# A new order and pace of the interleaved streams in a two-layer hybrid attention kernel

## The chip, the cores and the metric

One core of one Trainium2 chip. The metric is the device time of one execution in microseconds (us), the median over runs. The engines are TensorE (PE; its weight loads are PEld), VectorE (DVE), ScalarE (ACT), GpSimd (POOL, hardly used here) and SyncE (SP, on whose queue all loads and stores of this kernel are issued).

## The reference

A stack of two layers (D = 1024) over 512 latent tokens and 256 context tokens, weights shared between both. Each layer does this, and all of it is float32:

```python
h  = modulate(rms_norm(x, g_norm1[l]), sh1, sc1)      # latent; hc likewise from ctx
fl = stream_features(h, lw, rope)                     # one projection, split three ways
fc = stream_features(hc, lw, None)
mix_l, mix_c = token_mixers(fl, fc, lw, lam, lam_init, with_ctx_out)
x  = x + gt1 * (mix_l @ w_out[l])
x  = x + gt2 * swiglu(modulate(rms_norm(x, g_norm2[l]), sh2, sc2), w_gate, w_up, w_down)
```

`token_mixers` joins three groups of heads: four heads of latent attention with low-rank compressed q and kv (MLA), four heads of differential attention (softmax of one score matrix less lambda times softmax of a second), and eight heads of a bidirectional gated linear recurrence (HGRN) in chunks of 64 tokens, whose output is multiplied by a gate. Latent queries read context and latent keys; context queries read context alone. Layer 0 also computes the context's own output (`with_ctx_out`); layer 1 computes latent rows only.

## The kernel before

Activations lie transposed in SBUF, features on partitions and the 768 tokens along the free side (256 context, then 512 latent). Every float32 product is made of three fp32r matmuls, high*high, high*low and low*high (`gemm`, L189 to L198, the matmul is L195); so each weight block is fetched by SP into a staging tile `wst` (three buffers, L183), split by ACT into `whi` (L102) and by DVE into `wlo` (L105), and then used.

`phase_a(l, h, fs)` (L422) does everything of a layer up to the second norm. It runs four streams, each a Python generator that emits a piece of work and yields its estimated length:

- **g**, `stream_g`: the wide projections, in the order of the table `G_ORDER[l]`. `t0` to `t3` are the three HGRN projections of a pair of heads, `h0` and `h1` HGRN values, `q` differential q and k with rotary (DVE instructions of L105 on tiles `zt` and `raw_`), `d` differential values, `g0` to `g3` the HGRN gates (tanh on ACT, L105/L108 on DVE), `a4` to `a9` blocks of the modulation vector (their weights go through `wst` as well, L313). After them comes the output projection (L597 on).
- **h**, `stream_hh`: the recurrence, two heads at a time as two sub-streams. Its DVE work is the level products on tiles KK and QQ (L972), `copy_predicated` into the scores sc (L982), the chunk totals tot (L105), and the state scan sb (L108). A head pair's result is multiplied by its gate and stored in the scratch `scr_m`, slots 4 to 7; if the gate comes later than the pair, the `gate` step of g does it.
- **p**, `stream_p`: MLA compression, keys and values.
- **a**, `stream_a`, which starts when p has ended: softmax attention in items of 128 queries of one head. An item's scores (L775) go to a reduce on DVE (L779), an exponential on ACT into P, a reciprocal (L783), transposes of P on TensorE (L815), and the product with v (L829). Its results go to `scr_m`, slots 0 to 3. Attention units come in the order MLA context queries, MLA first latent batch, differential context, differential first latent batch, then the last 256 latent tokens.

Which stream emits next is decided by virtual time: each stream has a clock, the one furthest behind goes on, and its clock advances by the yielded length times the stream's pace. `PRM[l]` holds p's start offset and the paces of g, h, p and a. The tile scheduler then lays every engine's instructions out by priority, which falls with the order of emission; `AHEAD[l]` moves the priority of a stream's instructions by so many places. The order on each engine is fixed before the kernel runs.

The output projection goes over two batches of columns (layer 0: B1, the first 512 tokens, and B2, the last 256; layer 1: L1, latent tokens in the first 512 columns, and B2). For a batch it fetches two weight blocks, loads the eight slots of `scr_m` into one tile m2 as each becomes ready, and then makes eight column blocks:

```python
for k in (4, 5, 6, 0, 1, 2, 3, 7):
    yield from need(...)
    load(m2[:, k], scr_m[l][k, :, :, cols]...)
...
gemm(g[:, :n], w, [m2[:, :, i].bitcast(F32R) for i in range(2)], slice(0, n))
```

The matmuls take the slots in the order 0 to 7. For B2 the stream first waits for the end of stream a, so as to open its tile in the place that stream a's pool leaves.

After phase A come the feed-forward layer, then layer 1, then the final norm.

## Time and profile before

| | us |
|---|---|
| median of 3 runs | 2206.95 (2202.46 to 2211.0) |
| the profiled execution, its own time | 2209.03 |
| its span in the trace | 2206.9 |
| busy: TensorE, weight loads, VectorE, ScalarE | 2032.4, 1759.1, 1605.8, 1060.0 |
| mean granted clock of TensorE, share of full | 0.944 |
| layer 0's phase A | about 40 to 708 |
| layer 1's phase A | about 1280 to 1840 |

The profile comes from one execution; its span leaves out 2.1 us that the device's own time includes. A busy time is the time in which an engine has an instruction in hand, so a TensorE at a lower clock is busy for longer with the same work. The granted clock is the share of TensorE's full rate that the chip allowed in a stretch. Matmuls of one group overlap in the listing: starts are closer together than the lengths say.

### The profile page before, as it was taken

What the parts mean: (1) busy time and instruction counts of PE and PEld (TensorE: products, weight loads), DVE (VectorE), ACT (ScalarE), POOL (GpSimd) and SP (SyncE); (2) the same over time, 40 slices, a digit from 0 to 9 for tenths busy, and PEclk for the clock granted to TensorE, in tenths of its full rate; (3) what the DMA queues carried; (4) which work ended last, traced back from release to release, by engine and by line L of the source; (5) the groups of instructions that cost most, each with busy time, mean ns of one, the idle gap of its engine ahead of it and who ended that gap; (6) DMA issues with size and microseconds to landing.
All of it is one profiled execution on the core that took longest, in us unless ns stands there. A gap on an engine that the chain in (4) does not pass through costs nothing. (4 is left out here: it accounts for less than half of the span.)

```text
span 2206.9 us, 38015 instructions
## 1 busy us (share of the span) xinstructions
PE 2032.4 (92%) x14863; PEld 1759.1 (80%) x14863; DVE 1605.8 (73%) x3395; ACT 1060.0 (48%) x1871; POOL 13.1 (1%) x48
## 2 busy tenths in 40 slices
PE   7999899888898999999999999978988699999998
PEld 4887778666678888999999878757866489899997
DVE  5574597888657565797776776798568668877787
ACT  4433778565654323232333454445677444344443
POOL 0000000000000000000000000000000000000000
PEclk7999999888999999999999999989988589999999
DMA  9426744455765424464322333354645263333321
GB/s 318 122 77 165 196 131 131 128 164 170 223 203 167 125 86 153 129 187 132 118 70 68 118 114 102 95 150 128 171 129 163 83 204 98 96 105 101 103 85 68
DMA packets 321243, 296.51 MB, mean 134 GB/s; under 512 B 28875, under 2 KB 263721, under 8 KB 321065
## 3 DMA queue, kind: packets, MB, share of 16 engines
q1 hardware_dynamic: 321064, 294.10, 45.5%
q8 instruction: 117, 1.92, 0.4%
q14 instruction: 62, 0.50, 0.1%
HBM read 241.09 MB, written 52.95 MB: 133 GB/s over the span
## 5 line engine op out<-in xcount | busy, mean ns | idle before, releaser
L102 ACT ACTIVATE whi<-wst 128x1024 fp32r<-128x1024 f32 (+2 forms) x248 | 225.1, 908 | 399.9 <-PE f L195 146.4
L105 DVE TENSOR_TENSOR wlo<-wst,whi 128x1024 fp32r<-128x1024 f32 (+2 forms) x248 | 256.0, 1034 | 80.3 <-ACT whi L102 77.3
L195 PE MATMUL q<-hh,whi 128*128 128x384 f32 (+1 forms) x708 | 222.9, 317 | 4.3 <-ACT whi L102 3.2
L195 PE MATMUL q<-hh,wlo 128*128 128x384 f32 (+1 forms) x708 | 221.2, 315 | 0.9 <-DVE wlo L105 0.9
L195 PE MATMUL q<-hl,whi 128*128 128x384 f32 (+1 forms) x708 | 221.7, 314 | 0.0
L195 PE MATMUL g<-hh,whi 128*128 128x512 f32 (+1 forms) x560 | 199.6, 359 | 10.2 <-ACT zt L102 5.0
L195 PE MATMUL g<-hh,wlo 128*128 128x512 f32 (+1 forms) x560 | 197.8, 355 | 2.1 <-DVE wlo L105 2.1
L195 PE MATMUL g<-hl,whi 128*128 128x512 f32 (+1 forms) x560 | 198.9, 357 | 0.7 <-DVE hl L108 0.5
L195 PE MATMUL f<-ah,whi 128*128 128x512 f32 (+1 forms) x380 | 137.3, 364 | 5.3 <-DVE xT L108 4.1
L779 DVE TENSOR_REDUCE mx<-b 128x1 f32<-128x768 f32 (+1 forms) x120 | 101.5, 848 | 55.3 <-PE b L775 54.4
L195 PEld LDWEIGHTS q<-hh,whi 128*128 128x128 f32 x708 | 134.3, 190 | 9.1 <-ACT whi L102 5.1
L195 PE MATMUL f<-ah,wlo 128*128 128x512 f32 (+1 forms) x380 | 136.1, 361 | 1.1 <-DVE wlo L105 1.1
L195 PE MATMUL f<-al,whi 128*128 128x512 f32 (+1 forms) x380 | 136.5, 361 | 0.0
L108 DVE SCALAR_TENSOR_TENSOR xT<-f,mod,xT 128x256 f32<-128x256 f32 (+1 forms) x164 | 85.9, 546 | 69.1 <-PE f L195 68.5
L195 PEld LDWEIGHTS q<-hh,wlo 128*128 128x128 f32 x708 | 134.3, 190 | 1.7 <-DVE wlo L105 1.6
L195 PEld LDWEIGHTS q<-hl,whi 128*128 128x128 f32 x708 | 134.7, 191 | 0.3
L195 PEld LDWEIGHTS g<-hh,whi 128*128 128x128 f32 x560 | 108.1, 193 | 26.6 <-ACT zt L102 6.1
L102 ACT ACTIVATE kz<-KK 64x384 f32<-64x384 f32 (+1 forms) x192 | 91.3, 476 | 76.1 <-DVE KK L972 55.9
L775 PE MATMUL b<-k,q 96*128 96x256 f32 x352 | 100.5, 399 | 25.8 <-DMA q<-scr_d 15.6
L195 PEld LDWEIGHTS g<-hh,wlo 128*128 128x128 f32 x560 | 107.4, 192 | 17.2 <-DVE wlo L105 3.3
L195 PE MATMUL g<-T,whi 128*128 128x384 f32 (+1 forms) x544 | 121.1, 311 | 0.0
L195 PE MATMUL g<-m,whi 128*128 128x256 f32 (+1 forms) x512 | 117.2, 323 | 4.2 <-ACT acc L102 2.0
(308 smaller groups left out, 5021.2 us busy)
## 6 DMA issues: line engine op xcount, KB each, us to landing
wst<-in_w_in_dram SPq DMA_DIRECT2D x58, 512.0 KB, 5.3
wa<-in_w_ada_dram SPq DMA_DIRECT2D x56, 512.0 KB, 3.8
wst<-in_w_out_dram SPq DMA_DIRECT2D x32, 512.0 KB, 5.5
wst<-in_w_ffn_down_dram SPq DMA_DIRECT2D x64, 256.0 KB, 2.9
wst<-in_w_ffn_gate_dram SPq DMA_DIRECT2D x26, 512.0 KB, 3.7
wst<-in_w_ada_dram SPq DMA_DIRECT2D x24, 512.0 KB, 4.9
hin<-scr_z SPq DMA_DIRECT2D x48, 192.0 KB, 3.4
k<-scr_k SPq DMA_DIRECT2D x16, 576.0 KB
```

The source lines that it names most:

```text
L102: return S.activation(out=out, in_=in_, func=func, **kw)
L105: eng.tensor_tensor(out=out, in0=in0, in1=in1, op=op)
L108: return V.scalar_tensor_tensor(out=out, in0=in0, scalar=scalar, in1=in1, op0=op0, op1=op1)
L195: PE.matmul(out=o, lhsT=x[:, k, ms], rhs=y[:, k, cols], start=start and k == 0 and p == 0, stop=stop and k == nk - 1 and p == 2, skip_grou ...
L775: PE.matmul(out=s[:, 256 + k0:256 + k0 + kn], lhsT=qq[:, q0:q0 + 128], rhs=kk[:, k0:k0 + kn], start=p == 0, stop=p == len(passes) - 1)
L779: V.tensor_reduce(out=mx, in_=sv, axis=AX.X, op=ALU.min)
```

## The change

The tables that order the work have other numbers, and the output projection is written differently.

```diff
-G_ORDER = ("t0 h0 q t1 d t2 h1 t3 a5 a4 g0 a8 a6 g1 a9 a7 g3 g2", "t0 t1 h0 t2 q d h1 t3 g0 g1 g3 g2")
-PRM = ((40, 2, 2.1, 2, 1.2), (45, 1.8, 2.7, 2.2, 0.4))
+G_ORDER = ("t0 q t1 h0 d t2 h1 t3 a8 a5 a4 a6 g1 a9 g0 a7 g2 g3", "t0 h0 t1 t2 q d h1 g3 t3 g0 g1 g2")
+PRM = ((40, 2.4, 2.1, 2, 0.91), (35, 1.8, 2.7, 2.2, 0.4))
-AHEAD = ({}, {})
+AHEAD = ({'h': 0, 'a': 80}, {'a': 40, 'h': -40})
...
-                    if cols is B2:
+                    if cols is B2 and full:
                         yield from need("a")
                         op = apool.enter_context(tc.tile_pool(name=f"Q{l}", bufs=1, reuse_waits="tile"))
+                    order = [4, 5, 6, 0, 1, 2, 7, 3]
...
-                    m2 = op.tile([128, KT, 2, n], F32, name="m2")
-                    for k in (4, 5, 6, 0, 1, 2, 3, 7):
+                    m2 = op.tile([128, len(order), 2, n], F32, name=f"m2_{cols.start}")
+                    rows = {}
+                    for i, k in enumerate(order):
                         yield from need(...)
-                        load(m2[:, k], scr_m[l][k, :, :, cols].rearrange("i p t -> p i t"))
+                        load(m2[:, i], scr_m[l][k, :, :, cols].rearrange("i p t -> p i t"))
+                        rows[k] = [m2[:, i, e:e + 1].bitcast(F32R) for e in range(2)]
...
-                        gemm(g[:, :n], w, [m2[:, :, i].bitcast(F32R) for i in range(2)], slice(0, n))
+                        for k in rows:
+                            gemm(g[:, :n], [t[:, k:k + 1] for t in w], rows[k], slice(0, n), start=k == order[0], stop=k == list(rows)[-1])
```

In layer 0 the step `q` comes before `h0`, the modulation blocks a8 a5 a4 a6 follow one another, and the gates g0, g2 and g3 come later. In layer 1 `h0` comes before `t1` and the gate g3 before `t3`. Stream g's pace number in layer 0 goes from 2 to 2.4 (its clock runs faster, so it emits later), stream a's from 1.2 to 0.91 (it emits earlier). Stream p starts earlier in layer 1. In both layers stream a's instructions get a higher priority, in layer 1 those of h a lower one. Layer 1's second batch of the output projection no longer waits for stream a: it has a tile of its own beside the first batch's. The slots lie in the tile in the order of their loading, with 7 before 3, and the matmuls take them in that order, where they went from 0 to 7. A branch for a missing eighth slot is written too, which the order of eight slots never enters. The number of matmuls and of VectorE instructions is the same. The lines of the rest of the code lie seven further down (L779 becomes L786).

What moves is seen in the order of the instructions on an engine. VectorE, layer 1, where the first softmax reduce stands; before:

```order
L105 TENSOR_TENSOR zt<-zt,cosT 128x512
L972 TENSOR_TENSOR KK<-KK,tot 64x48x8
L105 TENSOR_TENSOR zt<-zt 128x512
L972 TENSOR_TENSOR QQ<-QQ,tot 64x32x8
L972 TENSOR_TENSOR KK<-KK,tot 64x48x8
L972 TENSOR_TENSOR QQ<-QQ,tot 64x32x8
L105 TENSOR_TENSOR zt<-zt 128x768
L105 TENSOR_TENSOR tot<-tot 128x48
L982 COPY_PREDICATED sc<-masks_75,c 64x4x64 x2
L779 TENSOR_REDUCE mx<-b 128x1
L972 TENSOR_TENSOR KK<-KK,tot 64x192x2
L779 TENSOR_REDUCE mx<-b 128x1
```

and now:

```order
L105 TENSOR_TENSOR zt<-g,sinT 128x512
L105 TENSOR_TENSOR zt<-zt,cosT 128x512
L105 TENSOR_TENSOR QQ<-hin 128x512
L105 TENSOR_TENSOR zt<-zt 128x512
L979 TENSOR_TENSOR KK<-KK,tot 64x96x4 x2
L786 TENSOR_REDUCE mx<-b 128x1 x2
L105 TENSOR_TENSOR zt<-zt 128x768
L105 TENSOR_TENSOR tot<-tot 128x96
L105 TENSOR_TENSOR tot<-hin 128x384
```

The head stream's products (L972, now L979) that stood ahead of the reduces (L779, now L786) have gone behind them.

VectorE, layer 0, among the softmax rows of MLA's first latent batch; before:

```order
L972 TENSOR_TENSOR QQ<-QQ,tot 64x96x4
L972 TENSOR_TENSOR KK<-KK,tot 64x96x4
L972 TENSOR_TENSOR QQ<-QQ,tot 64x96x4
L105 TENSOR_TENSOR tot<-tot 128x96
L982 COPY_PREDICATED sc<-masks_75,c 64x6x64 x2
L105 TENSOR_TENSOR mixs<-mix,mixs 128x256
L779 TENSOR_REDUCE mx<-b 128x1
L972 TENSOR_TENSOR QQ<-QQ,tot 64x192x2
L972 TENSOR_TENSOR KK<-KK,tot 64x192x2
L972 TENSOR_TENSOR QQ<-QQ,tot 64x192x2
L982 COPY_PREDICATED sc<-masks_75,c 64x6x64
L783 RECIPROCAL z<-z 128x1
```

and now:

```order
L105 TENSOR_TENSOR wlo<-wst,whi 128x1024
L786 TENSOR_REDUCE mx<-b 128x1
L105 TENSOR_TENSOR mixs<-mix,mixs 128x256
L786 TENSOR_REDUCE mx<-b 128x1
L790 RECIPROCAL z<-z 128x1
L105 TENSOR_TENSOR wlo<-wst,whi 128x1024
L790 RECIPROCAL z<-z 128x1
L786 TENSOR_REDUCE mx<-b 128x1
L790 RECIPROCAL z<-z 128x1
L786 TENSOR_REDUCE mx<-b 128x1
```

The reduces and reciprocals follow one another with split weights (wlo) and stored results (mixs) between them; the KK, QQ and sc rows of a head pair, which stood there, come later.

TensorE, layer 0, the last attention rows ahead of the output projection, whose rows are those on m; before:

```order
L775 MATMUL b<-k,q 128x256
L775 MATMUL b<-k,q 128x512
L775 MATMUL b<-k,q 128x256
L775 MATMUL b<-k,q 128x512
L815 MATMUL c<-ident,P 128x128 x12
L775 MATMUL b<-k,q 128x256
L775 MATMUL b<-k,q 128x512
L829 MATMUL c<-pt,v 64x256 x12
L195 MATMUL g<-m_6626,whi 128x512 x2
```

and now:

```order
L782 MATMUL b<-k,q 128x256
L782 MATMUL b<-k,q 128x512
L195 MATMUL g<-hh,wlo 128x256
L195 MATMUL g<-hh,whi 128x256
L195 MATMUL g<-hl,whi 128x256
L195 MATMUL g<-hh,wlo 128x256
L195 MATMUL g<-m_0_6743,whi 128x512 x2
L195 MATMUL g<-m_0_6743,wlo 128x512
L195 MATMUL g<-m_0_6743,whi 128x512 x2
L195 MATMUL g<-m_0_6743,wlo 128x512
L822 MATMUL b<-ident,P 128x128 x6
L782 MATMUL b<-k,q 128x256
```

Rows of a gate's projection (g from hh, hl) now stand among the scores (L775, now L782), and the first rows of the output projection (on m_0) come ahead of transposes and scores that in the order before had all gone by then.

## Rows read from the trace of the kernel before

**Rows 1.** The page: busy time of each engine, its share of the span, and instructions.

```profile
PE 2032.4 (92%) x14863; PEld 1759.1 (80%) x14863; DVE 1605.8 (73%) x3395; ACT 1060.0 (48%) x1871; POOL 13.1 (1%) x48
```

**Rows 2.** Stretches of layer 0's phase A: length, then busy time by engine, clock, DMA.

```profile
core 0: us, PE busy (x) PEld busy (x) DVE busy (x) ACT busy (x) POOL busy (x), PEclk, DMA share, GB/s
...
237.00:333.00 96.00, 91.60 (x961) 78.18 (x960) 71.16 (x157) 72.42 (x138) 0.59 (x4) 1.00 0.55 152
333.00:430.00 97.00, 91.38 (x926) 74.95 (x926) 78.31 (x213) 70.63 (x140) 0.58 (x4) 0.96 0.38 112
430.00:480.00 50.00, 40.49 (x366) 31.74 (x362) 35.39 (x87) 31.86 (x56) 0.29 (x2) 0.77 0.58 163
480.00:551.00 71.00, 59.43 (x620) 42.61 (x621) 61.90 (x147) 41.32 (x77) 0.29 (x2) 0.88 0.60 184
...
595.00:618.00 23.00, 12.76 (x53) 8.29 (x54) 12.06 (x21) 12.72 (x24) 0.00 (x0) 0.63 0.89 281
```

**Rows 3.** The same view, stretches of layer 1's phase A.

```profile
1440.00:1515.00 75.00, 56.06 (x466) 45.14 (x465) 65.43 (x143) 32.98 (x65) 0.29 (x2) 0.84 0.53 140
1515.00:1625.00 110.00, 107.42 (x849) 92.17 (x848) 71.53 (x150) 77.30 (x134) 0.29 (x2) 1.00 0.58 156
...
1690.00:1770.00 80.00, 50.89 (x363) 39.55 (x363) 56.04 (x141) 42.03 (x81) 0.03 (x1) 0.62 0.36 110
```

**Rows 4.** VectorE's groups by line, 1440 to 1515: count | busy, mean ns | idle.

```profile
L972 DVE TENSOR_TENSOR KK<-KK,tot 64x384 f32<-64x384 f32 x17 | 9.3, 550 | 0.2
L105 DVE TENSOR_TENSOR zt<-zt 128x512 f32<-128x512 f32 (+3 forms) x11 | 7.8, 706 | 0.2 <-ACT zt L102 0.2
L972 DVE TENSOR_TENSOR QQ<-QQ,tot 64x256 f32<-64x256 f32 x17 | 7.1, 417 | 1.3 <-PE c L931 1.0
...
L982 DVE COPY_PREDICATED sc<-masks,c 64x256 f32<-64x256 uint8 x12 | 5.3, 442 | 0.3
```

**Rows 5.** Chain of waits, 1440 to 1515, shares by line.

```profile
by line: DVE zt L105 18.7%; DVE KK L972 8.5%; issue 7.6%; PE c L931 7.4%; DVE QQ L972 5.5%; PE b L195 5.1%; DVE sb L108 4.9%; PE g L195 4.6%; DVE sc L982 4.6%; DVE tmp L105 3.7%; ACT zt L102 3.3%; DVE wlo L105 3.1%; DVE tot L105 2.9%; PE g 
```

**Rows 6.** VectorE's groups by line, 237 to 333.

```profile
L972 DVE TENSOR_TENSOR KK<-KK,tot 64x384 f32<-64x384 f32 x24 | 13.2, 552 | 1.3 <-PE c L944 0.8
...
L982 DVE COPY_PREDICATED sc<-masks,c 64x384 f32<-64x384 uint8 x20 | 11.8, 591 | 0.6
```

**Rows 7.** TensorE's timeline, 594 to 618: start, length, instruction, [idle before].

```profile
594.48 0.28 PE L195 MATMUL g<-hh,wlo 128*128 128x256 f32 x1
599.16 0.59 PE L775 MATMUL b<-k,q 96*128 96x256 f32 x2 [4.40 <-DMA q<-scr_d]
...
602.19 1.71 PE L775 MATMUL b<-k,q 96*128 96x256 f32 x4 [1.32 <-ACT P L102]
...
611.22 1.51 PE L815 MATMUL c<-ident,P 128*128 128x128 f32 x6 [2.96 <-DVE P L108]
...
617.77 0.74 PE L195 MATMUL g<-m,whi 128*128 128x512 f32 x2
```

**Rows 8.** Layer 1's second batch: SP's queue, the chain, TensorE, 1789 to 1808.

```profile
1789.99 5.16 SPq L411 DMA_DIRECT2D m<-scr_m  x8
...
1798.01 8.01 DMA wst<-in_w_out_dram
...
1798.00:1808.00 10.00, 7.77 (x61) 7.30 (x61) 5.18 (x12) 4.26 (x6) 0.00 (x0) 1.00 0.87 231
```

**Rows 9.** ScalarE's table loads: the group, and one with what follows it.

```profile
L102 ACT ACT_TABLE_LOAD x32 | 41.1, 1283 | 2.0 <-DVE mx L779 0.8 <-PEq L1592 0.7
...
364.04 1.28 ACT L102 ACT_TABLE_LOAD   x1
365.34 0.48 ACT L102 ACTIVATE P<-b,mx 128x256 f32<-128x256 f32 x1
```

**Rows 10.** Waits of 420 to 460, and the page's DMA issues: count, size, us to landing.

```profile
PEld g L313 <- DMA wst<-in_w_ada_dram: 3.2, 1, 3.2
...
wst<-in_w_ada_dram SPq DMA_DIRECT2D x24, 512.0 KB, 4.9
```

More of the change, by code (lines that the diff above doesn't have):

```diff
@@ L616, in stream_g @@
                             load(x[:, k:k + 2, qcols], scr_x[l][:, k:k + 2, qcols])
+                    if len(rows) < KT:
+                        yield from need(("m", 3, B2.start))
+                        rows[3] = [t.bitcast(F32R).unsqueeze(1) for t in last_rows]
                     add = sums(x, cols, np_)
```

## The prediction

> **What bounds the kernel now.** I read the engine totals first, then the two layers cut into stretches, then the waits inside the stretches that lose most. By the totals TensorE is busy for 92% of the span and VectorE for 73% [rows 1], so at most 8% can come from idle TensorE time as such. The cut by stretches shows that the loss is not even. In layer 0's phase A the stretches 237 to 333 and 333 to 430 are TensorE's: 91 us of work in 96 and 97 us. Then 480 to 551 has 59.4 us of TensorE work in 71 us with VectorE at 61.9, and 595 to 618 holds 12.8 us of TensorE work in 23 us, at a granted clock of 0.63, so that what little it does is done near the lower of the clock's two levels for much of the time [rows 2]. Layer 1 has the same picture: 1440 to 1515 has VectorE busy for 65.4 of 75 us (87%) and TensorE for 56.1, 1515 to 1625 is TensorE's (107.4 of 110), and 1690 to 1770 has 50.9 us in 80 at a clock of 0.62 [rows 3]. So a change of order can pay where VectorE is piled up in front of TensorE (1440 to 1515), and where the attention chain runs with nothing beside it (595 to 618 and 1690 to 1770). It can cost where it makes a new pile.
>
> **Layer 1, VectorE's pile.** In 1440 to 1515 the largest groups are the head stream's KK, QQ and sc instructions and the zt rows of the rotary step [rows 4], and the chain of waits in that stretch has VectorE's zt at 18.7% and KK at 8.5% ahead of any TensorE line [rows 5]. Of the head stream 309 VectorE instructions stand ahead of layer 1's first softmax reduce in the order before and 265 in the order now; by the durations of their own forms these 44 are 13 us (0.30 us each, since many are short tot rows; KK is 0.55 [rows 4]). Five rotary instructions at 0.70 us go behind as well: 4 us. Together 17 us leave: 65.4 − 17 = 48.4 us, which at the share of 87% needs 56 us instead of 75, a gain of 19. TensorE's own 56.1 us were run at a mean clock of 0.84; at full clock they would be between 47 (56.1 × 0.84) and 56, so I put the floor at 53. The 17 us come back in 1515 to 1625, where VectorE goes from 71.5 to 88.5 of 110 us [rows 3]; it has the room, but some of it will stand before an attention item, and I give back 5. Taken: **−14**. Ends: −22 (75 − 53, nothing given back) and +4 (only the head rows' 13 us are gained and all 17 are given back).
>
> **Layer 0, a new pile.** The same count of head instructions on VectorE ahead of the first item of differential attention (the stretch that begins at 333 us was cut there, [rows 2]) gives 228 before and 138 now. These 90 are 39 us by their forms (0.43 each, near sc and KK at 0.59 and 0.55 [rows 6]). In front of them nothing is won: 237 to 333 is already TensorE's with 4.4 us idle, so I allow −3 there. Behind them, lining both orders up by TensorE's work, 24 of the 39 us fall into what was 333 to 430, and the rest goes further on. That stretch has 78.3 us of VectorE beside 91.4 of TensorE [rows 2]; it would have 102.3 in 97 us. With VectorE never idle it is 5 us longer; at the 87% that VectorE reached in layer 1's pile [rows 3] it takes 117.6 us, 21 us longer. I take **+15**, nearer the second, since the only measured pile is that one. Ends: −3, and +38 if all 39 us fall there (117.3 / 0.87 = 134.8 us).
>
> **Layer 0's end.** From 594.5 to 617.8 the order before has nothing but attention rows on TensorE: it waits 4.4 us for q's transfer, 1.3 and 3.0 for P, and runs the rest near half clock [rows 7]. In the order now gate projections stand between the same rows, and the out-projection's first rows come before the last attention rows. The stretch's work at full clock is 12.8 × 0.63 = 8 us, so full cover is worth 23 − 8 = 15 us. The gates come from 430 to 551, which had VectorE, not TensorE, in front (480 to 551, 61.9 of 71 us [rows 2]), so I charge nothing there; if that cover is wrong, the upper end holds it. I take three quarters: **−11**. Ends: −15 and −3 (the q wait alone goes, and part of that).
>
> **Layer 1's second batch.** Before, its tile comes only after the attention stream's end, and the eight loads of m (5.2 us of the queue) stand between the weights of two column blocks; the next weights are waited for in the chain, 8.0 us from 1798.0, and TensorE is idle for 2.2 of the 10 us there [rows 8]. Now five of the eight stand ahead of the third weight block, and one and two more behind the last two stores. Nothing else is queued behind them but the weights. **−2**; ends −3.5 (the 2.2, and 1.3 for the two loads that are issued last now, 5.2 × 2/8) and +1, as the first weights now wait for five loads more.
>
> **Table loads.** The order now has six ACT_TABLE_LOAD fewer, two pairs in layer 0 and one in layer 1. Each is 1.28 us, and the next instruction starts 0.02 us after it [rows 9], so 7.7 us of ScalarE, which is busy for 48% [rows 1]. Two of them stand between a reduce and its P: **−2.6**; ends 0 and −7.7. The Trainium skill (ScalarE: Activation LUTs, What ACT_TABLE_LOAD costs) puts a switch at about 2.66 us, with a drain of 1.38 behind the load; by that the term would be an estimated −5.3, but these rows show no drain.
>
> **Modulation weights.** Four of the ada steps now follow one another; before, TensorE waits 3.2 us for such a load once, and a load lands 4.9 us after its issue [rows 10]. The new run of four could hide that wait, or make another one on the ring of three buffers: **−2**; ends −3 and +3.
>
> **The sum.** −14 + 15 − 11 − 2 − 2.6 − 2 = −16.6. The profiled execution took 2209.0 us with a span of 2206.9; the median of the three runs is 2207.0, 2.1 below it. On the median: 2207 − 16.6 = 2190, and I say 2191. A measurement of this kernel can tell about 0.5%, 11 us, from no change: faster lies below 2196, slower above 2218.
>
> **Rivals.**
> - *The new pile decides (slower).* All 39 us of head work fall before items of differential attention in 333 to 430: +38 instead of +15. TensorE's clock is granted by what it did before, so a waiting TensorE also loses rate (0.77 in 430 to 480, [rows 2]); and layer 1 gives back as much as +4 instead of −14 only if its pile moves too, of which I take a third (−8). 2190 + 23 + 6 = 2219. It decides as soon as more than 28 us of the 39 stand between the items of differential attention. For it: the orders, in which head rows that stood among the softmax rows of latent attention no longer do. Against: the heads' results are read by the out-projection only, at 617.8 us [rows 7], some 280 us later.
> - *The waits only move (no change).* 1690 to 1770 is an attention chain with almost nothing beside it, and its order there is as before. If the two piles end in a longer such chain, what is won early is waited for late; +15 stays, −14 and −11 shrink to −5 each: 2204. For it: the stretch is the emptiest of all [rows 3].
> - *Both piles thin out.* The moved head work finds the 19 us in which VectorE is idle in 333 to 430 and costs +2; layer 1 gains the full 22 and the end of layer 0 the full 15: −2 − 22 − 15 + 2 − 2.6 − 2 = −42, 2166. For it: VectorE's total is only 73%.
> - *A late slot holds TensorE.* Layer 0's out-projection takes each slot in the order in which it was loaded, the last gate's slot among the last, and the gates now end right ahead of it. TensorE has been seen waiting 4.4 us for a transfer with nothing run in its stead [rows 7]; tanh, product, split, store and load for the last slot make a chain of two transfers, 2 × 4.4, of which some 6 us can't be covered by the six slots before it. Then the end of layer 0 gains −3 instead of −11: 2199. The Trainium skill (PSUM — Partial Sum Buffer, Engine vs sequencer instructions) says that matmuls start and complete in program order, so that nothing behind a waiting one could pass it; by that rule the row would be general, and the trace agrees with its 4.4 us.
>
> **How the numbers follow.** My forecast has 0.45: its terms' middle halves give 2178 to 2204, two thirds of it below 2196. The new pile 0.18, waits only move 0.16, both thin out 0.12, the late slot 0.09. Faster: 0.31 + 0.12 + 0.04 of the others = 0.47; slower: 0.17 from the new pile; same: the remaining 0.36. The range reaches from 2166 a little down, 2164, to 2217: it leaves out the upper half of the new pile and a little at the other end.
>
> **What would show it.** The span of the stretch up to layer 1's first attention items shorter by some 15 us, VectorE no longer at 87% there; gate projections among layer 0's last attention rows and no wait of 4 us for q; a VectorE share of 90% and TensorE idle by 15 us in the second half of layer 0's attention; 26 table loads. The forecast is wrong if the middle of layer 0 costs nothing or over 28 us, or if layer 0's end still has a stretch at a clock near 0.6.

## The result, and the profile after

The changed kernel takes 2170.44 us (median of 4 runs, 2168.43 to 2172.47) where the kernel before took 2207.09 beside it: a ratio of 0.9826, with a 95% interval of 0.9802 to 0.985. That is 36.6 us less. The prediction named the direction and a range that holds the time (2164 to 2217), but its forecast of 16 us is less than half of what came.

The page of the changed kernel, its span, engine totals, and the granted clock in 40 slices:

```profile
span 2167.5 us, 37990 instructions
...
PE 2001.4 (92%) x14863; PEld 1737.5 (80%) x14863; DVE 1604.4 (74%) x3395; ACT 1051.5 (49%) x1859; POOL 13.1 (1%) x48
...
PEclk8999999989899999999999999999998799999999
```

Beside [rows 1], VectorE's total is unchanged, while TensorE is busy for 2001.4 instead of 2032.4 us with the same 14863 matmuls. The span is 39.4 us shorter. Of that, 31.0 us are TensorE busy time and 8.4 us are idle time (span less busy: 174.5 before, 166.1 now). No matmul went away, so the 31 us are matmuls that run at the upper level of the clock (2.4 GHz) where they ran at the lower one (1.2 GHz): by the clock records of the two traces, 184.4 us of the busy time lay at the lower level before and 111.6 us do now. The mean granted clock is 0.967, before 0.944.

To see where, I cut both executions at the same amount of TensorE work done, counting in each kernel's own order the columns of its matmuls; so each row of the first fence stands against the same row of the second. The borders agree to about 7000 of 3.9 million columns. Cut at exactly equal columns, the nine differences below are +12.1, −16.4, +7.6, −15.0 in layer 0 and −10.9, +1.2, −14.0, +1.5, −3.9 us in layer 1, so a single row is good to about 4 us. First layer 0, before (columns: stretch in us, its length, busy time of PE, PEld, DVE, ACT, POOL with counts, granted clock, DMA share, GB/s):

```profile
core 0: us, PE busy (x) PEld busy (x) DVE busy (x) ACT busy (x) POOL busy (x), PEclk, DMA share, GB/s
304.70:397.50 92.80, 90.45 (x962) 76.63 (x961) 73.56 (x189) 71.85 (x142) 0.54 (x4) 1.00 0.42 123
397.50:508.90 111.40, 88.97 (x870) 64.83 (x870) 90.61 (x225) 68.93 (x125) 0.34 (x3) 0.81 0.54 158
508.90:586.50 77.60, 72.01 (x664) 55.81 (x662) 54.01 (x129) 47.01 (x84) 0.29 (x2) 0.96 0.63 180
586.50:642.50 56.00, 45.34 (x227) 34.61 (x224) 35.22 (x70) 30.91 (x54) 0.00 (x0) 0.85 0.84 267
```

and after:

```profile
304.40:408.60 104.20, 94.57 (x989) 79.58 (x989) 90.24 (x235) 70.03 (x146) 0.58 (x4) 0.98 0.40 116
408.60:501.30 92.70, 81.55 (x885) 60.39 (x884) 82.20 (x207) 61.45 (x112) 0.58 (x4) 0.93 0.53 156
501.30:589.50 88.20, 77.82 (x691) 57.16 (x691) 66.26 (x148) 57.12 (x101) 0.29 (x2) 0.92 0.63 184
589.50:631.80 42.30, 39.94 (x233) 32.15 (x232) 27.73 (x62) 20.14 (x35) 0.00 (x0) 1.00 0.83 282
```

The first stretch is 11.4 us longer (92.8 to 104.2): VectorE's work in it rises from 73.6 to 90.2 us, 87% of the stretch. The second is 18.7 us shorter (111.4 to 92.7): VectorE's work falls from 90.6 to 82.2 us, TensorE's idle time from 22.4 to 11.2 us, and the clock rises from 0.81 to 0.93. The third and fourth together are 3.1 us shorter (133.6 to 130.5), with the work moved between them: the fourth runs at full clock now.

Then layer 1, before:

```profile
1402.40:1521.90 119.50, 99.03 (x861) 78.44 (x860) 102.76 (x223) 55.30 (x113) 1.02 (x7) 0.90 0.50 129
1521.90:1626.40 104.50, 102.22 (x798) 87.58 (x798) 65.82 (x138) 74.38 (x130) 0.15 (x1) 1.00 0.60 161
1626.40:1664.00 37.60, 31.71 (x234) 23.44 (x230) 28.96 (x79) 28.33 (x48) 0.29 (x2) 0.73 0.40 120
1664.00:1783.70 119.70, 87.27 (x677) 68.27 (x677) 83.69 (x212) 65.53 (x124) 0.29 (x2) 0.73 0.43 128
1783.70:1830.80 47.10, 43.75 (x349) 42.61 (x346) 34.75 (x70) 22.07 (x36) 0.00 (x0) 0.96 0.66 192
```

and after:

```profile
1390.30:1496.70 106.40, 91.74 (x749) 73.39 (x748) 93.49 (x205) 57.49 (x110) 0.87 (x6) 0.92 0.60 153
1496.70:1606.60 109.90, 105.24 (x891) 90.44 (x890) 76.88 (x172) 69.46 (x126) 0.29 (x2) 1.00 0.56 148
1606.60:1630.60 24.00, 23.21 (x214) 17.56 (x213) 20.01 (x57) 19.53 (x34) 0.29 (x2) 1.00 0.58 167
1630.60:1750.20 119.60, 84.55 (x702) 66.95 (x701) 89.66 (x230) 71.27 (x135) 0.29 (x2) 0.80 0.47 139
1750.20:1793.00 42.80, 41.19 (x347) 40.27 (x346) 35.02 (x72) 22.06 (x36) 0.00 (x0) 1.00 0.63 187
```

The first stretch, the pile of VectorE, is 13.1 us shorter, the second gives 5.4 back. VectorE has 9.3 us less work in the first, and its share there is still 88%. The third, of which the prediction said nothing, goes from 37.6 us at a clock of 0.73 to 24.0 us at full clock: 13.6 us. The fourth is the same, 119.7 and 119.6. The fifth, most of the output projection, is 4.3 shorter. These nine rows sum to −36.1 of the 39.4 us; the rest of the program gives 3.3. The last section shows how far such rows scatter in traces of the same order.

At the end of layer 0, the 23 us of [rows 2] and [rows 7] look like this now (the stretch, then the groups of TensorE by line, columns as in [rows 4]):

```profile
595.00:618.00 23.00, 21.74 (x130) 18.74 (x129) 17.53 (x28) 15.26 (x26) 0.00 (x0) 1.00 0.91 309
```

```profile
L195 PE MATMUL g<-hh,wlo 128*128 128x256 f32 (+1 forms) x24 | 7.7, 322 | 0.0
...
L822 PE MATMUL b<-ident,P 128*128 128x128 f32 x22 | 3.1, 275 | 1.3 <-DVE P L108 1.3
L782 PE MATMUL b<-k,q 96*128 96x256 f32 (+1 forms) x10 | 3.0, 376 | 0.0
```

Where 12.8 us of TensorE work stood at a clock of 0.63, there are 21.7 at full clock. Gate projections (g from hh and hl; 24 of the form shown) stand beside the attention rows, and no row there waits for q. The wait for a late slot, which one rival had, isn't seen.

### The profile page after: what moved, and what is told of

Its sections match the earlier page's. It is cut to its first block, busy times and chain, and to the rows that moved or that the text cites. A ratio compares the mean times of both kernels' runs of the same rounds, so it can differ in the third digit from the quotient of the medians.

```text
span 2167.5 us, 37990 instructions
## 1 busy us (share of the span) xinstructions
PE 2001.4 (92%) x14863; PEld 1737.5 (80%) x14863; DVE 1604.4 (74%) x3395; ACT 1051.5 (49%) x1859; POOL 13.1 (1%) x48
## 5 line engine op out<-in xcount | busy, mean ns | idle before, releaser
L195 PE MATMUL q<-hh,whi 128*128 128x384 f32 (+1 forms) x708 | 222.2, 316 | 4.3 <-ACT whi L102 3.2
L195 PE MATMUL q<-hh,wlo 128*128 128x384 f32 (+1 forms) x708 | 220.5, 314 | 0.9 <-DVE wlo L105 0.9
L195 PE MATMUL q<-hl,whi 128*128 128x384 f32 (+1 forms) x708 | 220.8, 313 | 0.0
L195 PE MATMUL g<-hh,whi 128*128 128x512 f32 (+1 forms) x560 | 200.0, 359 | 8.9 <-ACT zt L102 3.7
L195 PE MATMUL g<-hl,whi 128*128 128x512 f32 (+1 forms) x560 | 198.0, 355 | 0.8 <-DMA scr_x<-xT 0.5
L195 PE MATMUL g<-hh,wlo 128*128 128x512 f32 (+1 forms) x560 | 197.7, 355 | 0.8 <-DVE wlo L105 0.8
L786 DVE TENSOR_REDUCE mx<-b 128x1 f32<-128x768 f32 (+1 forms) x120 | 101.2, 848 | 56.4 <-PE b L782 55.1
L195 PE MATMUL f<-ah,whi 128*128 128x512 f32 (+1 forms) x380 | 137.2, 364 | 6.0 <-DVE xT L108 4.1
L195 PEld LDWEIGHTS q<-hh,whi 128*128 128x128 f32 x708 | 133.6, 189 | 9.2 <-ACT whi L102 5.1
L195 PE MATMUL f<-ah,wlo 128*128 128x512 f32 (+1 forms) x380 | 136.1, 361 | 1.1 <-DVE wlo L105 1.1
L195 PE MATMUL f<-al,whi 128*128 128x512 f32 (+1 forms) x380 | 136.5, 361 | 0.0
L195 PEld LDWEIGHTS q<-hh,wlo 128*128 128x128 f32 x708 | 133.6, 189 | 1.7 <-DVE wlo L105 1.6
L195 PEld LDWEIGHTS q<-hl,whi 128*128 128x128 f32 x708 | 133.9, 190 | 0.3
L195 PEld LDWEIGHTS g<-hh,whi 128*128 128x128 f32 x560 | 108.0, 194 | 25.4 <-ACT zt L102 5.3
L195 PEld LDWEIGHTS g<-hl,whi 128*128 128x128 f32 x560 | 107.4, 192 | 18.2 <-issue 2.7
L782 PE MATMUL b<-k,q 96*128 96x256 f32 x360 | 93.3, 371 | 30.3 <-DMA q<-scr_d 17.6
L195 PE MATMUL g<-T,whi 128*128 128x384 f32 (+1 forms) x544 | 121.1, 311 | 0.0
L195 PEld LDWEIGHTS g<-hh,wlo 128*128 128x128 f32 x560 | 107.2, 192 | 16.1 <-issue 1.7
```

What stands on the lines that cost most here:

```text
L195: PE.matmul(out=o, lhsT=x[:, k, ms], rhs=y[:, k, cols], start=start and k == 0 and p == 0, stop=stop and k == nk - 1 and p == 2, skip_grou ...
L782: PE.matmul(out=s[:, 256 + k0:256 + k0 + kn], lhsT=qq[:, q0:q0 + 128], rhs=kk[:, k0:k0 + kn], start=p == 0, stop=p == len(passes) - 1)
L786: V.tensor_reduce(out=mx, in_=sv, axis=AX.X, op=ALU.min)
```

## The experiments

All are the kernel before, or the changed kernel, with a part of the change put in or taken out; ratios are against the kernel before on the same chip. A lower ratio is faster; 0.005 is 11 us. Two kernels are told apart when their intervals are.

**First, the parts that the change consists of.** The three tables (`G_ORDER`, `PRM`, `AHEAD`) have an entry for each layer, and the output projection is separate code.

*Layer 0's tables alone* (l0_tables) and *layer 1's tables alone* (l1_tables), on the kernel before:

```diff
# l0_tables: entry 0 of the three tables as in the change, entry 1 as before
+G_ORDER = ("t0 q t1 h0 d t2 h1 t3 a8 a5 a4 a6 g1 a9 g0 a7 g2 g3", "t0 t1 h0 t2 q d h1 t3 g0 g1 g3 g2")
+PRM = ((40, 2.4, 2.1, 2, 0.91), (45, 1.8, 2.7, 2.2, 0.4))
+AHEAD = ({'h': 0, 'a': 80}, {})
# l1_tables: the other way round
+G_ORDER = ("t0 h0 q t1 d t2 h1 t3 a5 a4 g0 a8 a6 g1 a9 a7 g3 g2", "t0 h0 t1 t2 q d h1 g3 t3 g0 g1 g2")
+PRM = ((40, 2, 2.1, 2, 1.2), (35, 1.8, 2.7, 2.2, 0.4))
+AHEAD = ({}, {'a': 40, 'h': -40})
```

> The kernel before with layer 0's part of the three tables alone (step order, paces, priorities); layer 1 and the output projection as before. Theory A, the layers are separate and each table moves time within its own layer: 11 us faster than before (2196), since the changed kernel reached layer 0's feed-forward part 11 us earlier. Rival, my own sum: +15 for the pile of head work, -11 for the end, and about -4 for table loads and modulation weights, so no change (2207). If the output projection's new form carries layer 0's gain, this kernel is also at 2207.

> The kernel before with layer 1's part of the three tables alone. Theory A: 13 us from VectorE's pile at 1440 to 1515, less 6 given back, and 14 from the stretch 1625 to 1690 whose clock was below full: 21 to 24 us faster than before (2184). Rival: the stretch after 1625 is won by the output projection's second batch no longer waiting for the attention stream, then this kernel wins only 7 to 10 us (2198).

*The output projection alone* (out_only: the kernel before with the second half of the diff) and *without it* (no_out: the changed kernel with the old projection):

> The kernel before with the new output projection alone (tile of its own for layer 1's second batch, slots in the order of loading); all tables as before. Theory A: only the last 6 us of layer 1's gain are its own, and layer 0's projection gains 1 to 2: 2201. Rival: without the tables the last gate's slot comes late and the in-order matmuls on it wait, so no change (2207) or 3 us slower.

> The changed kernel with the output projection of before. Theory A: it loses what the part alone gains, 4 to 6 us of 36.6: 2176. Rival: the two parts need one another (the tables put the gates where only the new slot order can use them), then it loses 12 us or more (over 2182).

| kernel | median, us | ratio, 95% interval |
|---|---|---|
| l0_tables | 2193.87 | 0.9928 (0.9902 to 0.9954) |
| l1_tables | 2185.10 | 0.9899 (0.9867 to 0.9931) |
| out_only | 2202.26 | 0.9963 (0.9947 to 0.9980) |
| no_out | 2174.72 | 0.9831 (0.9801 to 0.9862) |
| all (the change) | 2170.44 | 0.9826 (0.9802 to 0.9850) |

Layer 0's tables gain 16 us, layer 1's 22, and the two add up to what both give (no_out, 37). So the layers are separate, as theory A had it (with 11 us for layer 0), and my sum of zero for layer 0 falls. The new output projection gains 8 us alone, a little over theory A's 6, but taking it out of the changed kernel can't be told from no change (0.9831 beside 0.9826), which neither theory had: what it gains by itself, the tables win as well.

**Layer 0's tables, part by part.**

```diff
# l0_order: entry 0 of G_ORDER alone
+"t0 q t1 h0 d t2 h1 t3 a8 a5 a4 a6 g1 a9 g0 a7 g2 g3"
# l0_pace: entry 0 of PRM alone
+(40, 2.4, 2.1, 2, 0.91)
# l0_prio: entry 0 of AHEAD alone
+{'h': 0, 'a': 80}
# l0_order_pace: the first two
```

> The kernel before with layer 0's new step order alone (paces and priorities as before). Theory C, the clock: layer 0's tables won 16 us because the stretch 425 to 512 no longer runs at 0.64 to 0.84 of the clock; the step order, which takes a gate out of the modulation blocks and puts them one after another, is what closes it, so it gives most: 8 to 12 us faster (2199). Rival D, the pace of the streams is what does it: this kernel is within 4 us of before.

> The kernel before with layer 0's new paces alone (attention emitted earlier, projections later). Theory C: the projections left over for the end of layer 0 fill the attention rows there, 5 to 8 us faster (2203), and the pile of head work at 333 to 430 stays small. Rival D: 12 us or more (2197).

> The kernel before with layer 0's new step order and paces, without its new priorities. Alone the order cost 15 us and the paces 9. Theory E, order and paces complete one another (the paces leave projections for the end of the layer, the order puts q ahead so that attention has them, and gates last so that there is filler): together they give most of the 16 us, 10 to 16 us faster (2197). Rival F, the attention stream's priority is the third leg: without it the pair stays within 5 us of before (2209).

> The kernel before with layer 0's new priority (attention ahead by 80 places) alone. Theory E: within 5 us of before. Rival F: it carries the gain, 8 us or more faster (2201).

| kernel | median, us | ratio, 95% interval |
|---|---|---|
| l0_order | 2227.41 | 1.0067 (1.0049 to 1.0084) |
| l0_pace | 2220.44 | 1.0040 (1.0023 to 1.0056) |
| l0_prio | 2221.55 | 1.0046 (1.0021 to 1.0070) |
| l0_order_pace | 2201.92 | 0.9960 (0.9940 to 0.9980) |
| l0_tables (all three) | 2193.87 | 0.9928 (0.9902 to 0.9954) |

Neither theory's numbers held for a single part: each of the three alone makes the kernel slower, by 15, 9 and 10 us. Order and paces together gain 9, between theories E and F, and all three gain 16, though the intervals of these two overlap. Where the paces alone lose is seen in one stretch: with attention emitted earlier in the old step order, TensorE waits for tiles zt of VectorE and of ScalarE, and needs 37.7 us for an amount of work that took the kernel before 24.4 (208.8 to 233.2). The stretch of l0_pace, and its longest waits (engine, line waited for: us in total, times, longest):

```profile
212.30:250.00 37.70, 25.57 (x110) 20.52 (x108) 16.76 (x24) 15.26 (x27) 0.00 (x0) 0.82 0.60 161
...
PE b L195 <- DVE zt L105: 6.0, 1, 6.0
PE g L195 <- ACT zt L102: 3.8, 1, 3.8
```

With `q` ahead of `t1` and `h0` in the step order this stretch has its projections, and the pair no longer loses there.

The priority's part is seen in the two stretches of layer 0's middle, cut as above. The pair without it (l0_order_pace):

```profile
308.70:404.30 95.60, 92.59 (x961) 78.13 (x961) 80.97 (x218) 68.11 (x141) 0.59 (x4) 1.00 0.43 122
404.30:513.90 109.60, 91.99 (x890) 65.06 (x890) 86.06 (x212) 66.35 (x120) 0.58 (x4) 0.83 0.55 161
```

The priority alone (l0_prio):

```profile
305.10:407.40 102.30, 94.73 (x1027) 79.29 (x1024) 85.48 (x216) 72.82 (x151) 0.59 (x4) 0.98 0.42 124
407.40:512.60 105.20, 87.90 (x827) 64.29 (x826) 82.43 (x205) 67.33 (x118) 0.29 (x2) 0.84 0.49 144
```

Before they were 92.8 and 111.4 us, with all three 103.0 and 92.4 in l0_tables. The pair leaves the second stretch at 109.6 us and a clock of 0.83. The priority alone lengthens the first to 102.3 and leaves the second at 105.2, at 0.84, though VectorE has the same 82 us there as in the changed kernel. So most of the longer first stretch is the priority's doing. What shortens the second isn't settled: the paces alone, with neither the new step order nor the priority, already bring it to 97.4 us at a clock of 0.93. They lose that again in the stretch behind it, which took 77.6 us before, and in the one ahead that was shown above (l0_pace, the second stretch and the one behind it, cut at equal columns):

```profile
419.70:517.10 97.40, 84.60 (x911) 64.08 (x910) 87.83 (x216) 68.75 (x125) 0.58 (x4) 0.93 0.45 132
517.10:609.30 92.20, 78.25 (x652) 55.21 (x652) 59.96 (x143) 51.74 (x93) 0.29 (x2) 0.91 0.64 184
```

With all three entries the one ahead loses nothing, and the two behind take 130.5 us together (133.6 before), where the paces alone take 141.3. VectorE's load by itself doesn't decide it (87.8 us here, 82.4 with the priority alone), which speaks against reading a stretch by one engine's total.

*The modulation blocks and gate g0 back in their old places* (ada_old), on the changed kernel:

```diff
-"t0 q t1 h0 d t2 h1 t3 a8 a5 a4 a6 g1 a9 g0 a7 g2 g3"
+"t0 q t1 h0 d t2 h1 t3 a5 a4 g0 a8 a6 g1 a9 a7 g2 g3"
```

> The changed kernel with layer 0's modulation blocks and gate g0 in the old places (a5 a4 g0 a8 a6 g1 a9 a7), gates g2 and g3 as in the change. Theory J: the 20 us of the stretch 430 to 510 come from there, and this kernel is 8 to 20 us slower than the changed one (2183). Rival K: they are the price of the pile paid back (the head rows that were pushed behind 260 to 320 of the attention no longer stand there), which stays as it is: within 5 us (2173).

It took 2187.54 us, 0.9892 (0.9871 to 0.9914): about 15 us slower than the changed kernel by the ratios. But the place is not the one expected. The second stretch of layer 0's middle is as in the change, within 1.0 us, so rival K holds for it. The loss lies after it, where the gate that went forward is missing at the end (562.7 to 601.8 takes 39.1 us, in the changed kernel the same work took 29.1, from 560.4 to 589.5):

```profile
562.70:601.80 39.10, 32.45 (x230) 21.82 (x229) 21.08 (x64) 17.27 (x31) 0.00 (x0) 0.83 0.58 172
601.80:652.00 50.20, 44.71 (x227) 35.08 (x226) 29.94 (x57) 23.61 (x38) 0.00 (x0) 0.89 0.92 290
```

TensorE is idle for 6.7 us of the first row and runs at 0.83. It has 24 matmuls of a gate's projection (g from hh and hl) there, where the changed kernel has 55 in its 29.1 us. That a gate kept for the end fills this place fits, but this kernel also moves the modulation blocks, and no run parts the two.

**Layer 1's tables, part by part.**

```diff
# l1_order: entry 1 of G_ORDER alone
+"t0 h0 t1 t2 q d h1 g3 t3 g0 g1 g2"
# l1_prio: entry 1 of AHEAD alone
+{'a': 40, 'h': -40}
# l1_offset: entry 1 of PRM alone
+(35, 1.8, 2.7, 2.2, 0.4)
# l1_offset_order: offset and order
```

> The kernel before with layer 1's new step order alone. Theory C: the step order (one head step earlier, one gate before the last projections) gives less than half of the 22 us of layer 1's tables: 4 to 9 us faster (2203). Rival D: it gives nearly all of them, 18 us or more (2191).

> The kernel before with layer 1's new priorities alone (attention ahead by 40 places, the recurrence behind by 40). Theory C: this is what takes the head rows from in front of the softmax reduces on VectorE, and so wins the 12 us of 1440 to 1515: 10 to 15 us faster (2197). Rival D: alone it only turns the pile round, so that the recurrence ends later and the output projection waits for it: within 4 us of before.

> The kernel before with the compression stream's start offset of layer 1 alone (45 to 35). Theory H: this, not the priorities, puts the first softmax reduce ahead of the head rows, so the stretch 1440 to 1515 gives its 13 us, of which 6 go back by 1625, and what follows is as before: 5 to 10 us faster (2202). Rival: with the old step order the earlier attention finds no projections to stand beside it, as layer 0's paces alone showed, and the kernel is 5 us slower or more (2215).

> The kernel before with offset and step order of layer 1, without its priorities. Theory H: 13 less 6 from the pile and 11 from the step order, 16 to 22 us faster (2191). Rival: the priorities are the third leg, as in layer 0, and without them it is 12 us or less (over 2198).

| kernel | median, us | ratio, 95% interval |
|---|---|---|
| l1_order | 2200.20 | 0.9942 (0.9919 to 0.9965) |
| l1_prio | 2207.73 | 0.9976 (0.9957 to 0.9995) |
| l1_offset | 2221.61 | 1.0054 (1.0038 to 1.0070) |
| l1_offset_order | 2208.18 | 0.9976 (0.9961 to 0.9991) |
| l1_tables (all three) | 2185.10 | 0.9899 (0.9867 to 0.9931) |

The step order alone gains 13 us, between the two theories, and the priorities 5, nearer to rival D. The start offset alone costs 12, as the rival had it, although it does by itself what the prediction's largest term described: cut by TensorE's work, l1_offset needs 107.0 us (1405.0 to 1512.0) for the stretch that took 119.5 before, where l1_order and l1_prio need 118 and 120. The loss comes at the end, where the old output projection waits for slots and the attention rows for q (waits of l1_offset from 1755 to 1825):

```profile
PE g L195 <- DMA m<-scr_m: 8.2, 1, 8.2
PE b L775 <- DMA q<-scr_d: 5.4, 1, 5.4
```

The stretches after the pile tell the parts apart as well. From 1626.4 to 1783.7 before (157.3 us) l1_order gains 11.5 us, l1_prio 1.5, and l1_offset loses 2.2; l1_tables gain 8.6 and the change 13.7. So the step order is what wins there. With the offset beside it the gain is gone (0.3 us in l1_offset_order, which then loses 9 in the output projection: 71.9 us from its first to its last matmul on m, before 62.5) and comes back only with the priorities. So offset and order without them gain 5 us, not the 16 to 22 expected: the rival with a third leg held.

*Gate g3 of layer 1 back behind the last projections* (g3_late), and two tries to go further the same way, all on the changed kernel:

```diff
# g3_late, layer 1
-"t0 h0 t1 t2 q d h1 g3 t3 g0 g1 g2"
+"t0 h0 t1 t2 q d h1 t3 g0 g1 g3 g2"
# g1_later, layer 0
-"t0 q t1 h0 d t2 h1 t3 a8 a5 a4 a6 g1 a9 g0 a7 g2 g3"
+"t0 q t1 h0 d t2 h1 t3 a8 a5 a4 a6 a9 g1 a7 g0 g2 g3"
# g3_earlier, layer 1
-"t0 h0 t1 t2 q d h1 g3 t3 g0 g1 g2"
+"t0 h0 t1 t2 q d h1 g3 g0 t3 g1 g2"
```

> The changed kernel with layer 1's gate g3 put back behind the last projections and g0, g1. Theory I: g3's early place gives the 10 us behind 1625, so this kernel is 6 to 12 us slower than the changed one (2180). Rival: it is h0's earlier place that gives them, then within 4 us of the changed kernel (2172).

> The changed kernel with one more gate of layer 0 moved late: g1 stands behind modulation block a9 and g0 behind a7. Theory L: what a gate is worth is that its matmuls stand beside the last attention items, so one more helps again, 4 to 8 us faster than the changed kernel (2166). Rival M: the end is filled already (TensorE is busy for 21.7 of 23 us from 595 to 618 at full clock), and the modulation blocks lose their cover: 3 to 10 us slower (2178).

> The changed kernel with gates g3 and g0 of layer 1 both ahead of the last HGRN projections (g3 g0 t3 g1 g2). Theory L for layer 1: a gate in front lets the projections t3 stand later beside attention, 3 to 7 us faster (2167). Rival M: t3's head pair starts later, the recurrence is what the output projection waits for, and the kernel is 3 to 10 us slower (2178).

g3_late took 2177.25 us, 0.9850 (0.9833 to 0.9868), g1_later 2177.13, 0.9829 (0.9789 to 0.9868), g3_earlier 2189.17, 0.9890 (0.9867 to 0.9914). The intervals of the first two overlap that of the changed kernel, so by the times what g3's place is worth stays open, as does g1's. The trace of g3_late says where it could lie, in the third and fourth stretch of layer 1:

```profile
1606.80:1632.10 25.30, 22.72 (x189) 17.36 (x188) 22.26 (x61) 22.57 (x38) 0.29 (x2) 1.00 0.47 137
1632.10:1757.10 125.00, 91.63 (x700) 70.44 (x698) 89.12 (x225) 69.22 (x132) 0.29 (x2) 0.75 0.45 136
```

The third is nearly as short as in the change (24.0), the fourth 5.4 us longer (119.6). g3_earlier is about 14 us slower than the change, more than rival M had. No further step of this kind was found to win.

**The clock by itself.** Two kernels add matmuls whose result nothing reads, so as to keep TensorE occupied in layer 1's last attention items (warm4 with 4, warm8 with 8 behind each score map; written as a loop here, without the lines that count the maps in sc1 and keep the order's priorities as they were):

```diff
+for _ in range(8 if sc1[0] > 16 else 0):
+    PE.matmul(out=s[:, 0:256], lhsT=passes[0][0][:, q0:q0 + 128], rhs=passes[0][1][:, 0:256], start=True, stop=True)
 sv = s[:, 256:256 + nk]
```

> The changed kernel with four matmuls of 256 columns more, whose result nothing reads, behind each of the last 16 score maps of layer 1's differential attention: 64 matmuls, some 8 us of TensorE work at full clock, put where the clock is 0.77 and 0.71. Theory C, the time lost there is TensorE's lower clock: the clock in the stretch before the output projection rises over 0.85 and the stretch gets shorter by 3 to 6 us in spite of the added work (2166). Rival G, the stretch is a chain through VectorE, ScalarE and the q loads, and the low clock is a consequence of it only: the clock rises and the time stays or grows by 2 to 6 us (2174).

> The same with eight matmuls: 128 of them, 16 us of work. Theory C: the clock in that stretch is over 0.9 and the time 4 to 8 us shorter than the changed kernel's (2164). Rival G: longer by 4 to 12 us (2178).

They took 2182.77 us, 0.9870 (0.9840 to 0.9899), and 2184.12, 0.9876 (0.9844 to 0.9908), about 10 us over the changed kernel by the ratios, though the intervals of both still touch its own (up to 0.9850). The stretch from the first of these sixteen score maps to the last, of the changed kernel, of warm4 and of warm8:

```profile
1667.40:1738.30 70.90, 47.99 (x371) 38.76 (x372) 50.56 (x133) 38.69 (x76) 0.00 (x0) 0.72 0.35 104
```

```profile
1669.90:1756.30 86.40, 66.60 (x485) 55.41 (x486) 54.52 (x138) 40.54 (x80) 0.00 (x0) 0.73 0.38 115
```

```profile
1662.90:1754.20 91.30, 74.46 (x552) 65.41 (x553) 57.74 (x140) 42.21 (x81) 0.00 (x0) 0.76 0.39 114
```

TensorE is busy for 68, 77 and 82% of it, and the granted clock is 0.72, 0.73 and 0.76. It hardly rose, so what both theories took for granted fell, and theory C's gain with it: the stretch is 15.5 and 20.4 us longer. The added instructions also changed the order of what follows, so these are not all theirs. That the low clock of this stretch can be bought off with filler is not shown; that it costs something there isn't shown by these runs either.

## Why the prediction was right or wrong, point by point

| term of the sum | forecast, us | measured in its stretch, us |
|---|---|---|
| layer 1, VectorE's pile | −14 | −13.1 and +5.4 given back: −7.7 |
| layer 0, a new pile | +15 | +11.4 where it stands, −18.7 behind it: −7.3 |
| layer 0's end | −11 | −3.1 with the stretch before it |
| layer 1's second batch | −2 | −4.3 |
| layer 1 from 1626 on | none | −13.6, −0.1 |
| table loads, modulation weights | −4.6 | 7.7 less of ScalarE and 0.4 less of waits; what they bring is not told apart from the rest |

**The step that failed** is the one on layer 0's new pile. It read "24 of the 39 us fall into what was 333 to 430, and the rest goes further on", and priced only the place where the rows were to arrive. Here is the stretch behind that place as it was before, and then both as they are now, cut at equal columns of TensorE work (333 to 430 before is in [rows 2]):

```profile
430.00:551.00 121.00, 99.92 (x986) 74.35 (x983) 97.29 (x233) 73.18 (x133) 0.58 (x4) 0.83 0.59 175
```

```profile
337.50:438.80 101.30, 94.63 (x964) 79.26 (x961) 87.47 (x229) 66.16 (x131) 0.58 (x4) 0.98 0.43 120
438.80:544.90 106.10, 92.00 (x1037) 67.13 (x1035) 91.09 (x214) 75.95 (x134) 0.58 (x4) 0.94 0.60 174
```

The place of the forecast is 4.3 us longer (97.0 to 101.3), not 15, and no head work fell into it. VectorE's groups there, before and now:

```profile
L972 DVE TENSOR_TENSOR KK<-KK,tot 64x384 f32<-64x384 f32 x23 | 12.7, 551 | 0.5
...
L982 DVE COPY_PREDICATED sc<-masks,c 64x384 f32<-64x384 uint8 x20 | 11.8, 589 | 0.5
L779 DVE TENSOR_REDUCE mx<-b 128x1 f32<-128x256 f32 (+1 forms) x19 | 9.6, 508 | 5.4 <-PE b L775 5.2
...
L108 DVE SCALAR_TENSOR_TENSOR P<-P,z 128x256 f32<-128x256 f32 x8 | 3.8, 479 | 0.3
```

```profile
L786 DVE TENSOR_REDUCE mx<-b 128x1 f32<-128x768 f32 (+1 forms) x18 | 13.3, 744 | 7.2 <-PE b L782 7.2
L979 DVE TENSOR_TENSOR KK<-KK,tot 64x384 f32<-64x384 f32 x24 | 13.2, 552 | 0.5
...
L989 DVE COPY_PREDICATED sc<-masks,c 64x384 f32<-64x384 uint8 x18 | 10.6, 590 | 0.4
...
L108 DVE SCALAR_TENSOR_TENSOR P<-P,z 128x768 f32<-128x768 f32 (+1 forms) x9 | 7.0, 777 | 0.3
```

The KK rows are one more and the sc rows two fewer. VectorE's 9.2 us more (78.3 to 87.5) are softmax rows of larger score maps (mx and P) and weight splits. The 39 us were counted against the first item of differential attention, and that mark itself moved: its first reduce starts at 333.9 us before and at 293.7 now. Against TensorE's work only 8 us of head rows went behind the border at 333 (104.1 us of VectorE rows on KK, QQ, sc, tot, sb and hin stood ahead of it, 95.9 do now). So attention went ahead by far more than head work went back.

What was left out is the place behind, the slowest of layer 0's middle. I said of it in another paragraph that it had VectorE in front, and charged and credited it with nothing. It is 14.9 us shorter (121.0 to 106.1): TensorE's idle time there falls from 21.1 to 14.1 us and the clock rises from 0.83 to 0.94. So the step had the wrong sign. With the borders of the first fences the term is −7.3, with these −10.6, and by its own sign ("wrong if the middle of layer 0 costs nothing") the forecast fell. l0_tables shows this as a whole, 16 us faster where my sum for layer 0 was about zero. That the first stretch of the first fences reached VectorE's 87%, as assumed, and cost 11.4 us, near 15, is in good part luck: it is not the stretch that was priced. Which of the rows that moved makes the place behind shorter stays open, since the paces alone do it too (97.4 us).

**A second term was missing.** I had noted that the order in 1690 to 1770 didn't change and stopped there. The stretch ahead of it (37.6 us, clock 0.73) held TensorE idle for 5.9 us and kept it at the lower clock for much of the rest, though no wait in it is long (the longest is 1.4 us). It went to 24.0 us at full clock. l1_order, the step order alone, gains 11.5 us over this stretch and the next, l1_prio 1.5. In l1_prio, cut at equal columns, this stretch is short too (24.7 us), but the next takes 130.8. So of the two it is the order, with h0 and g3 moved, that keeps the gain. g3's early place is not what fills the stretch itself, which is 25.3 us in g3_late; h0's place was not tried alone.

**Layer 1's pile** was read rightly in place, and its size was about half: 19 less 5 was forecast, 13.1 less 5.4 came. 17 us of VectorE work were to leave the stretch, and 9.3 left (102.8 to 93.5). VectorE's share stayed (86% before, 88% now), as the working had it; the sign that it would no longer be at 87% did not come. The prediction left open which edit moves it; l1_offset shows that the start offset does, not the priorities, to which I put it afterwards.

**Layer 0's end** was right in mechanism. TensorE is now busy for 21.7 of the 23 us from 595 to 618 at full clock, with gates among the attention rows. Its size was not: the 13.7 us won from 586.5 on are mostly paid for in the stretch ahead (+10.6), which I had charged nothing. That the gates were missing there as cover is not shown, since it has 105 matmuls of gate projections now and had 108. What it has more is VectorE work (54.0 to 66.3 us) and waits in the modulation step (3.8 us on L313 and L321, none there before). ada_old shows the worth of the end from the other side: with a gate fewer there, and the modulation blocks in their old order, the kernel is 15 us slower.

**The small terms.** There are 26 table loads where 32 stood, at the same 1283 ns each:

```profile
L102 ACT ACT_TABLE_LOAD x26 | 33.4, 1283 | 1.9 <-DMA hin<-scr_z 0.8 <-PEq L1599 0.7
```

The group fell by 7.7 us (41.1 to 33.4), as the rows said, and ScalarE's busy total by 8.5 (1060.0 to 1051.5). The Trainium skill (ScalarE: Activation LUTs, What ACT_TABLE_LOAD costs) puts a switch at about 2.66 us, its drain included; by that the six would be an estimated 16 us of ScalarE time. This case's trace doesn't bear that out: in the kernel before, 24 of the 32 loads are followed by the next instruction within 0.02 us, and 31 of them start within 0.02 us of the end of the one before.

The wait for the modulation blocks' weights hardly changed. Over layer 0's phase A (40 to 715 us) TensorE's matmuls wait for them twice before and four times now:

```profile
PE g L313 <- DMA wst<-in_w_ada_dram: 3.2, 2, 2.8
```

```profile
PE g L313 <- DMA wst<-in_w_ada_dram: 2.8, 4, 1.5
```

The run of four blocks shortened the one long wait of [rows 10] and made shorter ones in other places.

**The rivals.** The new pile did not decide, and the waits did not only move. "Both piles thin out" gave 2166, nearest to the time, but not by its own steps: layer 0's middle was to cost 2 and gained 7.3, layer 1's pile was to give 22 and gave 7.7, layer 0's end 15 and gave 3.1. That the range held the time is therefore luck in part. The late slot held nothing up. (Two of the rivals' times are added up 1 us off: the waits that only move come to 2205, both piles thinned out to 2165.)

**The clock's share.** I had worked each term out as time in a stretch, so the clock was in it, but never asked of the sum how much of the loss was clock. With 31.0 of 39.4 us the larger part of the gain is matmuls that run faster, not gaps that closed. The two are not independent: the rows with a low clock are those in which TensorE was also idle for long (22.4 us at 0.81 in layer 0's middle, 32.4 at 0.73 in layer 1's fourth stretch), so the split says where the time went and not what the clock alone cost. In the same way no_out has an idle time of 166.3 us, within 0.2 of the changed kernel's, and l0_tables and l1_tables 171.1 and 170.4 with 12.3 and 19.6 us less busy time than before.

## What to carry to other kernels

When work is moved behind other work, price three places: where it leaves, where it arrives, and the slow stretch after that; the last was worth more here than the second. Count what moves against the work of the busiest engine, not against a mark that the change moves as well: 39 us of head work had gone behind the first item of differential attention, and 8 us behind the same TensorE work. Cutting two executions at equal work done on the busiest engine shows each of these as a row, where cutting at equal times smears them. Parts of a schedule can't be judged alone: layer 0's three entries cost 15, 9 and 10 us one by one and gained 16 together, so a search that changes one at a time would have refused each.

## What the runs showed of the hardware that was not expected

The granted clock hardly followed how busy TensorE was in layer 1's last attention items: 0.72 with 48.0 us busy of 70.9, 0.73 with 66.6 of 86.4, 0.76 with 74.5 of 91.3. A matmul at the lower level takes longer (a 128x512 one of L195 has a median of 628 ns there and 389 at the upper level, in the kernel before), so part of a high busy share is the low clock itself.

A piece of the same order mostly takes the same time, and in one place it doesn't. The five kernels with parts of layer 1's tables run layer 0 in the order of before on every engine, and the five with parts of layer 0's tables run layer 1 so; g3_late, g3_earlier, warm4 and warm8 keep the changed layer 0, ada_old the changed layer 1. Cut at the same instructions, the nine rows take:

| stretch before, us | order of before, 6 traces | order of now, 5 traces in layer 0, 2 in layer 1 |
|---|---|---|
| 304.7 to 397.5 | 92.5 to 92.6 | 102.9 to 104.1 |
| 397.5 to 508.9 | 109.7 to 115.9 | 91.7 to 92.9 |
| 508.9 to 586.5 | 75.1 to 77.8 | 87.6 to 88.2 |
| 586.5 to 642.5 | 55.0 to 57.1 | 42.0 to 42.7 |
| 1402.4 to 1521.9 | 117.7 to 120.3 | 106.1 to 106.3 |
| 1521.9 to 1626.4 | 104.4 to 106.0 | 109.9 to 110.4 |
| 1626.4 to 1664.0 | 37.2 to 37.6 | 24.0 to 24.1 |
| 1664.0 to 1783.7 | 119.7 to 121.0 | 119.6 to 120.6 |
| 1783.7 to 1830.8 | 46.8 to 47.2 | 42.7 to 42.8 |

So all of the rows but the eighth are the order's, the output projection's 4.3 us too. The widest scatter, 6 us, is that of the slow stretch of layer 0 in the order before. What the third and fourth row give together is small, but stands out: 130.7 to 134.1 us before, 129.8 to 130.3 now.
